# Layer 0's entry, reordered: token tiles turned first, the first head group summed by pairs of K-slices, and two tiles of the second head group summed ahead of the scores

## The chip, the cores and the metric

The kernel runs on one core of one Trainium2 chip. The metric is the device time of one execution in microseconds (us); of the kernel before there are three runs, 1695.23, 1698.65 and 1695.23 us, with a median of 1695.23. The profile is of one more execution on the chip. Engines in the rows: PE (TensorE), PEld (its weight loads), DVE (VectorE), ACT (ScalarE), POOL (GpSimd), SP (SyncE, which issues nearly all loads).

## The reference

Two layers of a transformer block over 512 latent tokens and 256 context tokens of width 1024. Layer 0 has four groups of heads (two with a window, two dense); each group has four query heads, one key head and one value head of width 64. What the change touches is the way into layer 0:

```python
mx = (s_c @ mod_w[l] + mod_b[l])[:, None, :]          # shift, scale, gate ... of the latent tokens
mc = (s_cc @ mod_w[l] + mod_b[l])[:, None, :]         # the same of the context tokens
hx = _rms(x, norm_mix_w[l]) * (1.0 + scx1) + shx1
hc = _rms(ctx, norm_mix_w[l]) * (1.0 + scc1) + shc1
...
qa_x, ka_x, va_x, ... = heads(hx @ w_in, True)        # then RMS norm and rotation of q and k
qa_c, ka_c, va_c, ... = heads(hc @ w_in, False)
```

The change leaves out nothing and computes nothing else.

## The kernel before

**Tiles.** The 768 tokens are six tiles of 128 rows: 4 and 5 are the context, 0 to 3 the latent tokens, taken in the order `CTX_FIRST = (4, 5, 0, 1, 2, 3)`. The width of 1024 is eight K-slices of 128, taken as four pairs. A float32 product is made of three products of rounded parts (high x high, high x low, low x high), so `project` (L465) issues, for one tile and one pair of K-slices, 2 x 3 matmuls of 128x384: the 384 columns are 4 query heads, a key head and a value head. A tile of one head group is 24 matmuls, a head group 144.

**The entry, L1149 to L1214.** `load_x` loads a tile of tokens (512 KB). Its square sum is made on ACT (L1166), the inverse root on POOL (L159, L160), the scaling on DVE (L1167); PE turns it in eight transposes of 128x128 (L1171) into two PSUM banks, and ACT copies both halves into `xT` (L1172). There are two buffers `nh` for the scaled tile, so the third tile's square waits until the first tile has been turned. Beside that, `mod_steps` makes the shift (part 0) and the scale (part 1) of layer 0: for each of four chunks n of 256 columns (two K-slices) and each part it loads two pieces of 512 KB, multiplies them (16 matmuls for a chunk, L182), copies the rows (`modr`, ACT, L185), turns them into columns (L191), and adds them on DVE (L276, L280). `modulated(k)` applies them to a K-slice on DVE (L1184), ACT makes the high part (L1189), DVE or, for the context tokens, POOL the low part (L1190). `weights0` does the same for the weights: a pair of K-slices is three loads (`wir`), a cast on ACT (`wihi`, L498) and a subtraction on DVE or POOL (`wilo`, L499). `start_tile` hands out six buffers under the tag `mw` to mod pieces and to weights; `raw_tile` two others.

**The order.** PE's order is written out by hand between `manual.__enter__` and `manual.__exit__` (first L1176 to L1214); outside, and on the other engines, the scheduler of the language orders instructions by its own timeline, and every engine and SP's queue then run strictly in that order. In the written part, tiles 4 and 5 get all 24 matmuls once all four chunks are on their way. After it the scheduler places the four other tiles.

**What follows.** `in_proj0` copies a summed tile out (`qkv`, ACT, L520), squares it (L440), sums by head (DVE, L442), takes the inverse root on POOL (`rs_q`, L159, L160), multiplies by it on POOL (L523), splits q and k (`qd`, `kd`: ACT L525, L529, DVE L526, POOL L530) and queues two transposes on PE (`turn_q`, `turn_k`, L535, L543). `attend0` then makes scores (`sc`, L578), the softmax and the values. While head group b attends, `quarters` places the products of head group b+1 between its steps, by the table `QUARTS`; one quarter is one pair of K-slices of one tile.

## Time and profile before

| | us |
|---|---|
| three runs | 1695.23, 1698.65, 1695.23 (median 1695.23) |
| span of the profiled execution | 1695.6 |
| PE busy / DVE / ACT / POOL in it | 1631.5 / 1146.7 / 937.0 / 696.4 |
| first product of the first head group begins | 42.91 |
| first scores begin | 77.39 |

The profiled execution's own time is its span, 0.4 us above the median; what else a run's time takes in is not listed. Times below are us from the start of that span. In a row of the timeline stand the start, the length, the engine, the line, the operation, what it writes and reads, the shape and the count; a matmul's length is its way through the array, and matmuls overlap, so their pace is read from starts and counts. In a row of the windows stand the stretch, its length, busy time and count of PE, PEld, DVE, ACT, POOL, then the clock granted to PE (1.00 is full), the busy share of the transfer engines and GB/s.

### The profile page before, as it was taken

The numbers are of one execution on the slowest core, as the hardware profiler recorded it, in microseconds if no ns is written. First come the engines' busy times: TensorE is split into PE (matmuls) and PEld (weight loads), VectorE is DVE, ScalarE is ACT, GpSimd is POOL, SyncE is SP. The second block draws the span as 40 slices with busy tenths as digits, with TensorE's granted clock in tenths as the row PEclk, the third lists the DMA queues.
The fourth block names the chain that finished last, engine by engine and source line by source line (L and its number), as shares of the span: only waits on it lengthen the run. The fifth ranks groups of instructions, "written<-read, shape, count | busy, mean of one in ns | idle before, by whom it ended". The sixth has DMA issues, their size and how long they took to land. (4 is left out here: it accounts for less than half of the span.)

```text
span 1695.6 us, 28585 instructions
## 1 busy us (share of the span) xinstructions
PE 1631.5 (96%) x10390; PEld 1468.6 (87%) x10390; DVE 1146.7 (68%) x2014; ACT 937.0 (55%) x2011; POOL 696.4 (41%) x867
## 2 busy tenths in 40 slices
PE   6999999899999999999999989999999999999998
PEld 3977787677999999998777889999988899999887
DVE  3765656754799887767767656666666598887434
ACT  5565555745456665545554456666666555555320
POOL 2665554321346554412413366666664242221000
PEclk8999999999999999999999999999999999999999
DMA  9222221411455555439966311111112433331431
GB/s 319 69 71 74 70 70 50 164 60 38 129 167 172 164 159 162 134 108 347 296 184 189 99 43 38 48 42 44 50 45 97 125 93 102 111 101 57 137 99 62
DMA packets 218108, 194.64 MB, mean 115 GB/s; under 512 B 20016, under 2 KB 202864, under 8 KB 217968
## 3 DMA queue, kind: packets, MB, share of 16 engines
q1 hardware_dynamic: 217616, 192.62, 36.8%
q8 instruction: 81, 1.33, 0.3%
q14 instruction: 59, 0.48, 0.1%
q10 hardware_dynamic: 352, 0.21, 0.0%
HBM read 179.92 MB, written 12.87 MB: 114 GB/s over the span
## 5 line engine op out<-in xcount | busy, mean ns | idle before, releaser
L901 ACT CAST wbh<-wr 128x512 fp32r<-128x512 f32 x170 | 104.9, 621 | 130.2 <-PE p L933 73.4
L933 PE MATMUL p<-hT,wbh 128*128 128x256 f32 (+1 forms) x752 | 154.5, 299 | 0.0
L465 PE MATMUL inps<-wih,hT 128*128 128x384 f32 x512 | 144.2, 344 | 7.3 <-ACT qkv L677 7.3
L911 POOL TENSOR_TENSOR wbl<-wr,wbh 128x512 fp32r<-128x512 f32 x43 | 60.0, 1396 | 173.6 <-ACT wbh L901 173.6
L933 PEld LDWEIGHTS p<-hT,wbh 128*128 128x128 f32 x752 | 121.9, 191 | 0.2
L911 DVE TENSOR_TENSOR wbl<-wr,wbh 128x512 fp32r<-128x512 f32 x127 | 107.7, 858 | 21.0 <-ACT wbh L901 16.8
L933 PE MATMUL p<-hT,wbl 128*128 128x256 f32 (+1 forms) x376 | 111.9, 298 | 0.0
L933 PE MATMUL p<-t,wbh 128*128 128x384 f32 (+1 forms) x480 | 111.3, 318 | 0.0
L604 POOL TENSOR_SCALAR Pt<-Pt,rc 128x256 f32<-128x256 f32 (+3 forms) x96 | 74.6, 788 | 89.3 <-DVE rc L601 83.1
L231 POOL TENSOR_TENSOR modp<-modp 128x512 f32<-128x512 f32 x40 | 57.4, 1436 | 114.3 <-ACT modp L230 114.3
L465 PEld LDWEIGHTS inps<-wih,hT 128*128 128x128 f32 x512 | 93.3, 188 | 10.6 <-ACT qkv L677 9.7
L933 PE MATMUL p<-hTt,wbh 128*128 128x256 f32 (+1 forms) x480 | 101.0, 302 | 0.0
L887 POOL TENSOR_TENSOR wr<-wr 128x512 f32<-128x512 f32 x40 | 61.6, 1540 | 89.8 <-DVE ws L892 85.8
L933 PE MATMUL p<-b,wbh 128*128 128x384 f32 x368 | 93.8, 336 | 0.2 <-DVE c L961 0.2
L901 ACT CAST wbh<-ws 128x512 fp32r<-128x512 f32 x120 | 69.4, 579 | 43.1 <-PE p L933 29.0
L224 DVE SCALAR_TENSOR_TENSOR ma<-modw,cols,ma 128x256 f32<-128x256 f32 x140 | 89.2, 637 | 2.3
L592 ACT ACTIVATE Pt<-sc,nm 128x256 f32<-128x256 f32 (+3 forms) x96 | 67.6, 707 | 35.3 <-DVE nm L588 16.9
L465 PE MATMUL inps<-wil,hT 128*128 128x384 f32 x256 | 86.0, 336 | 0.0
L933 PEld LDWEIGHTS p<-t,wbh 128*128 128x128 f32 x480 | 82.9, 189 | 0.0
L911 DVE TENSOR_TENSOR wbl<-ws,wbh 128x512 fp32r<-128x512 f32 x120 | 81.7, 681 | 1.7 <-ACT wbh L901 1.6
L933 PEld LDWEIGHTS p<-hTt,wbh 128*128 128x128 f32 x480 | 78.3, 191 | 3.1 <-ACT modp L230 1.6
L230 ACT ACTIVATE modp<-modw,cols 128x256 f32<-128x256 f32 x160 | 68.4, 500 | 18.0 <-POOL ma L236 10.1
(355 smaller groups left out, 5217.9 us busy)
## 6 DMA issues: line engine op xcount, KB each, us to landing
modw<-in_mod_w_dram SPq DMA_DIRECT2D x96, 512.0 KB, 5.2
wr<-in_ffn_w_in_dram SPq DMA_DIRECT2D x176, 256.0 KB, 2.9
wdr<-in_ffn_w_out_dram SPq DMA_DIRECT2D x66, 512.0 KB, 3.7
wir<-in_od_w_in_dram SPq DMA_DIRECT2D x96, 128.0 KB, 2.3
hidm<-hid SPq DMA_DIRECT2D x44, 192.0 KB, 1.9
hr<-hidm SPq DMA_DIRECT2D x22, 192.0 KB, 3.5
x<-in_x_dram SPq DMA_DIRECT2D x8, 512.0 KB, 3.5
wir<-in_ev_w_in_dram SPq DMA_DIRECT2D x16, 256.0 KB, 3.5
```

The source lines that it names most:

```text
L224: nc.vector.scalar_tensor_tensor(acc, w[:, k], scale[k], acc, ALU.mult, ALU.add)
L230: nc.scalar.activation(pr[:, k], w[:, k], AF.Copy, scale=scale[k])
L231: nc.gpsimd.tensor_add(pr[:, 0:2], pr[:, 0:2], pr[:, 2:4])
L465: nc.tensor.matmul(ps, hs[j][:, k, :], ws[k // 2][z][:, k % 2, c0:c1], start=(k, j, z) == (0, 0, 0), stop=(k, j, z) == (KT - 1, 1, 0))
L592: turn["exp"] = nc.scalar.activation(p[:, :n], s, AF.Exp, bias=nm[:, c1], accum_out=sm[:, c1])
L604: nc.gpsimd.tensor_scalar(p[:, :n], p[:, :n], rc[:, hh:hh + 1], 1.0, ALU.mult, ALU.mult)
L887: nc.gpsimd.tensor_sub(w, raw[f, "G1"], w)
L901: nc.scalar.copy(hi, w)
L911: (nc.gpsimd if name == "G2" else nc.vector).tensor_sub(lo, raw[need[n]], f32(hi))
L933: nc.tensor.matmul(ps, w[:, k, :], H[b][h][:, k, :], start=first and k == 0 and q == 0, stop=final and k == 3 and q == 2, skip_group_check ...
```

## The change

The change does the following.

- All six token tiles are loaded ahead of the first mod piece and turned one after the other; the second half of each is copied by DVE and no longer by ACT.
- PE's order is written out by hand from the first transpose on. For each chunk n: its 16 matmuls, its columns, `modulated(n, i)` for the context and the latent tokens, all low parts on DVE, and then the pair of K-slices n of the six tiles. Chunk n+1's matmuls and columns stand between the products of chunk n. Four tiles begin in new places (`acc0`, `acc1` for tiles 4 and 5, the two score buffers for 0 to 3).
- The weights of a pair are loaded one pair at a time, between the chunks' pieces. `mw` has seven buffers; one pair of pieces (chunk 2, part 1) goes to the raw buffers.
- Head group 1's first weights are asked for in the third round; its tiles 4 and 5 are summed in the written part, ahead of the scores, each followed by the transposes of two tiles of head group 0. `QUARTS` for head group 0's attention then places 16 quarters in place of 24.
- The rotation tables and the sinks are placed behind the last low part and the last mod piece.

```diff
+MW = 7
-    def start_mod(n):
-        for part in range(2):
-            mod_chunk(0, part, n, start_tile, start.pool, f"acc{part}", p_sc)
...
+    def chunk_rows(n):
+        chunks[n] = [mod_steps(0, part, n, raw_tile if n == 2 and part else start_tile, start.pool, f"{'tr' if n else 'tr'}{part}", room=("modr", 2))
+                     for part in range(2)]
+        for g in chunks[n]:
+            next(g)
...
-            nc.scalar.copy(xT[:, 4 * g:4 * g + 4, t * P:(t + 1) * P], pt)
+            (nc.vector.tensor_copy if g else nc.scalar.copy)(xT[:, 4 * g:4 * g + 4, t * P:(t + 1) * P], pt)
...
-                (nc.gpsimd if s0 else nc.vector).tensor_sub(lo, xT[:, ks, s0:s1], f32(hi))
+            turn["lows"] = nc.vector.tensor_sub(lo, xT[:, kk, s0:s1], f32(hi))
...
+    xs.update({t: load_x(t) for t in CTX_FIRST[2:]})
+    for t in CTX_FIRST:
+        turned_x(t)
+    chunk_rows(0)
+    units = weights0(0, wp.pool, (nc.vector,), start_tile, ((0,), (1,), (2,), (3,)), True)
+    next(units)
+    chunk_columns(0)
+    for i in (1, 0):
+        modulated(0, i)
+    ws.append(next(units))
...
+    begin(0, *CTX_FIRST[:2])
+    for n in range(1, 4):
+        chunk_rows(n)
+        next(units)
+        if n == 3:
+            units1 = weights0(1, wp.pool, (nc.gpsimd, nc.vector))
+            next(units1)
+        begin(n - 1, *CTX_FIRST[2:4])
+        chunk_columns(n)
+        with behind("lows"):
+            ws.append(next(units))
+        for i in (1, 0):
+            modulated(n, i)
+        begin(n - 1, *CTX_FIRST[4:])
+        begin(n, *CTX_FIRST[:2])
+    with behind("lows"):
+        ws1 = [next(units1) for _ in range(2)]
+    begin(3, *CTX_FIRST[2:])
...
-    for _ in range(2 * NT):
-        quarters(2)
-        turned0()
+    for _ in range(4 * NT):
+        next(proj)
+    ws1 += units1
+    proj = in_proj0(1, ws1, tabs, wp.pool, odd.pool, due)
+    nxt = next(proj)
+    for _ in range(2):
+        for _ in range(4):
+            next(proj)
+        for _ in range(4):
+            due.pop(0)()
+    manual.__exit__(None, None, None)
...
-    QUARTS = ((((2, 2),) * 6), ((2, 2),) * 6, ((2, 2), (2, 2), (4, 2), (2, 4), (2, 2), (0, 0)))
+    QUARTS = (((1, 1), (1, 1), (2, 1), (2, 1), (2, 1), (2, 1)), ((2, 2),) * 6, ((2, 2), (2, 2), (4, 2), (2, 4), (2, 2), (0, 0)))
```

Line numbers of the changed kernel are higher by one up to the entry (L465 becomes L466) and by 7 to 22 behind it.

**PE, the opening.** In the kernel before, the transposes of the six tiles (`npt`), the chunks' matmuls (`mod`) and their columns (`modcol`) are mixed; the stretch from the last tile on reads:

```order
L1171 MATMUL npt<-cst,nh 128x128 x8
L191 MATMUL modcol<-cst,modr 128x2 x2
L182 MATMUL mod<-modw,s_pad 32x256 x12
L191 MATMUL modcol<-cst,modr 128x2 x2
L182 MATMUL mod<-modw,s_pad 32x256 x12
L191 MATMUL modcol<-cst,modr 128x2 x2
L182 MATMUL mod<-modw,s_pad 32x256 x8
L465 MATMUL inps<-wihi,hTc_112 128x384
```

In the changed kernel PE begins:

```order
L145 MATMUL pcol<-cst,rows 128x48
L149 MATMUL pb<-cst,brows 128x96
L1180 MATMUL npt<-cst,nh 128x128 x48
L183 MATMUL mod<-modw,s_pad 32x256 x16
L192 MATMUL modcol<-cst,modr 128x2 x4
L466 MATMUL inps<-wihi,hTc_112 128x384
```

All 48 transposes stand ahead of the first chunk, and the first product behind one chunk in place of four.

**ACT, the rounds.** Here `wihi` is the high part of a pair of weights and `wir` its load, `modr` the rows of a chunk, `hTc0` and `hT0` the high parts of the context and latent tokens. Before, from the second part of chunk 2's rows on:

```order
L185 COPY modr_357<-mod_344 128x256
L185 COPY modr_379<-mod_366 128x256
L498 CAST wihi_422<-wir_396 128x768
L1189 CAST hT0_110<-xT_210 128x512
L498 CAST wihi_436<-wir_400 128x768
L1189 CAST hTc0_112<-xT_210 128x512
```

In the changed kernel, from behind the first chunk's high parts to those of the third:

```order
L499 CAST wihi_377<-wir_352 128x768
L499 CAST wihi_470<-wir_445 128x768
L186 COPY modr_335<-mod_322 128x256
L186 COPY modr_350<-mod_337 128x256
L1191 CAST hTc0_112<-xT_124 128x512
L1191 CAST hT0_110<-xT_124 128x512 x2
L186 COPY modr_428<-mod_415 128x256
L186 COPY modr_443<-mod_430 128x256
L499 CAST wihi_571<-wir_538 128x768
L499 CAST wihi_609<-wir_542 128x768
L499 CAST wihi_613<-wir_546 128x768
L1191 CAST hTc0_112<-xT_124 128x512
```

The casts of the second and third pair (`wir_352`, `wir_445`) now stand ahead of chunk 1's rows; those of the fourth pair and of head group 1's first two (`wir_538`, `wir_542`, `wir_546`) ahead of chunk 2's high parts. SP issues `wir_445` into the buffer of `wir_352` and `wir_538` into that of `wir_445`, so each waits for the low part of the pair before it on DVE, and that stands behind the round's low parts of the tokens. `wir_542` and `wir_546` follow in SP's queue.

**POOL, the first tiles' rotation.** `qy` are the rotated heads of a tile, `rs_q` their inverse roots (two instructions, the second against `neghalf`), `kd` a tile's key. Before, from the first tile's inverse root to the second tile's key:

```order
L160 TENSOR_TENSOR rs_q_562<-rs_q_562,neghalf_92 128x5
L160 TENSOR_TENSOR rs_q_582<-rs_q_582,neghalf_92 128x5
L159 TENSOR_SCALAR rs_q_637<-qss_635 128x5
L523 TENSOR_TENSOR qy_565<-qy_565,rs_q_562 128x320
L523 TENSOR_TENSOR qy_585<-qy_585,rs_q_582 128x320
L160 TENSOR_TENSOR rs_q_637<-rs_q_637,neghalf_92 128x5
L530 TENSOR_TENSOR kd_572<-qy_565,kd_572 128x128
L499 TENSOR_TENSOR wilo_867<-wir_862,wihi_866 128x768
L530 TENSOR_TENSOR kd_592<-qy_585,kd_592 128x128
```

In the changed kernel, from the low part of head group 1's third pair to the second tile's key:

```order
L500 TENSOR_TENSOR wilo_809<-wir_804,wihi_808 128x768
L161 TENSOR_TENSOR rs_q_695<-rs_q_695,neghalf_92 128x5
L522 COPY vv_667<-qkv_732 128x64
L160 TENSOR_SCALAR rs_q_715<-qss_713 128x5
L531 TENSOR_TENSOR kd_685<-qy_678,kd_685 128x128
L160 TENSOR_SCALAR rs_q_739<-qss_737 128x5
L524 TENSOR_TENSOR qy_698<-qy_698,rs_q_695 128x320
L161 TENSOR_TENSOR rs_q_715<-rs_q_715,neghalf_92 128x5
L161 TENSOR_TENSOR rs_q_739<-rs_q_739,neghalf_92 128x5
L522 COPY vv_667<-qkv_756 128x64
L524 TENSOR_TENSOR qy_718<-qy_718,rs_q_715 128x320
L531 TENSOR_TENSOR kd_705<-qy_698,kd_705 128x128
```

The low part of the weights has moved ahead of the second tile's inverse root, and two more inverse roots and a multiplication ahead of its key.

More of the change, by code (lines that the diff above doesn't have):

```diff
@@ L1192, in backbone, with begin @@
-    ws, begun, first = [], {}, CTX_FIRST[:2]
-    for k in range(6):
-        modulated(k)
-        if k % 2:
-            ws += islice(units, 1)
-    for i in range(0, 4, 2):
+        for kk in [slice(ks[0], ks[0] + 2)] if i else [slice(k, k + 1) for k in ks]:
+            hi, lo = (cols_T(j, s0, s1)[:, kk, :] for j in range(2))
+            turn["started"] = nc.scalar.copy(hi, xT[:, kk, s0:s1])
+            turn["lows"] = nc.vector.tensor_sub(lo, xT[:, kk, s0:s1], f32(hi))
+    def begin(n, *tiles):
+        for t in tiles:
+            project(begun[t], t, ws, 0, 384, range(2 * n, 2 * n + 2))
@@ L1198, in backbone @@
+    xs.update({t: load_x(t) for t in CTX_FIRST[2:]})
[8 more added lines that the diff above has]
+    ws.append(next(units))
+    for i, t in enumerate(CTX_FIRST[:2]):
+        begun[t] = acc_tile("inps", 384, one=i)
+    for i in range(2, 6, 2):
         sc = p_sc.pool.tile([P, 1024], F32, name="inps", tag="sc", bufs=2)
```

68 lines of the change are left out of this document (23 added, 45 removed).

## Prediction

> **What bounds the kernel now.** I read the page's slices first, then the windows, then PE's timeline of the entry. The page shows PE's busy tenths and its clock in 40 slices of 42.4 us:
>
> ```profile
> PE   6999999899999999999999989999999999999998
> PEclk8999999999999999999999999999999999999999
> ```
>
> PE is the bound everywhere but in the first slice. Only there and in the head groups behind it can this change act. The windows of that stretch:
>
> ```profile
> 0.00:20.00 20.00, 8.96 (x74) 4.60 (x74) 2.85 (x7) 10.79 (x21) 3.22 (x12) 1.00 0.96 327
> 20.00:40.00 20.00, 15.05 (x109) 9.87 (x110) 11.10 (x23) 11.10 (x23) 5.34 (x8) 0.68 1.09 329
> ...
> 0.00:42.90 42.90, 26.65 (x202) 15.76 (x202) 15.95 (x36) 23.77 (x46) 8.56 (x20) 0.82 1.00 319
> 42.90:77.40 34.50, 33.04 (x199) 32.22 (x195) 25.89 (x50) 16.93 (x38) 21.13 (x27) 0.98 0.28 81
> ...
> 80.00:100.00 20.00, 18.63 (x133) 15.85 (x132) 11.47 (x45) 12.74 (x42) 15.85 (x30) 1.00 0.17 57
> 100.00:120.00 20.00, 18.25 (x142) 14.55 (x140) 14.13 (x41) 13.88 (x37) 12.25 (x19) 1.00 0.33 93
> ```
>
> Up to 42.9 us the transfers run without a pause (share 1.00, 319 GB/s) and PE does 26.65 us of work, partly at a low clock. From 42.9 to the first scores at 77.4 PE is busy 33.04 of 34.5 us, and behind that it idles 1.4 to 1.8 us in 20. So the entry waits for loads, and then PE has everything it needs. PE's timeline:
>
> ```profile
> 11.28 1.06 PE L1171 MATMUL npt<-cst,nh 128*128 128x128 f32 x4
> ...
> 14.85 1.07 PE L182 MATMUL mod<-modw,s_pad 128*32 128x256 f32 x16
> ...
> 20.36 1.94 PE L1171 MATMUL npt<-cst,nh 128*128 128x128 f32 x8 [2.74 <-DVE modc L276]
> ...
> 26.81 1.94 PE L1171 MATMUL npt<-cst,nh 128*128 128x128 f32 x8 [1.05 <-DVE nh L1167]
> 28.68 1.08 PE L182 MATMUL mod<-modw,s_pad 128*32 128x256 f32 x8
> 29.69 1.50 PE L1171 MATMUL npt<-cst,nh 128*128 128x128 f32 x8
> ...
> 37.91 1.94 PE L182 MATMUL mod<-modw,s_pad 128*32 128x256 f32 x16 [1.12 <-DVE modc L276]
> ...
> 42.91 1.56 PE L465 MATMUL inps<-wihi,hTc 128*128 128x384 f32 x4
> 44.30 0.50 PE L191 MATMUL modcol<-cst,modr 128*128 128x2 f32 x4
> ...
> 77.39 0.70 PE L578 MATMUL sc<-kT,qt 128*128 128x256 f32 x4
> ```
>
> The most that could be won is what PE loses up to 77.4: 17.7 us idle (77.4 - 26.65 - 33.04) and some 8 us of low clock.
>
> **Step 1: the transposes first.** They no longer share PE with the chunks, but a tile's loop is a chain: square, inverse root, scaling, eight transposes, and two tiles are in flight (two buffers `nh`).
>
> ```profile
> 6.59 1.04 ACT L1166 ACTIVATE nh<-x 128x1024 f32<-128x1024 f32 x1
> ```
>
> ```profile
> 8.68 0.75 DVE L1167 TENSOR_SCALAR nh<-x,rs_n 128x1024 f32<-128x1024 f32 x1 [1.08 <-POOL rs_n L160]
> ...
> 40.83 0.16 DVE L276 TENSOR_TENSOR modc<-modcol,bcol 128x4 f32<-128x4 f32 x1 [2.97 <-PE modcol L191]
> 41.22 1.65 DVE L1184 TENSOR_SCALAR xT<-xT,aff,modc 128x256 f32<-128x256 f32 x4
> 42.79 0.95 DVE L499 TENSOR_TENSOR wilo<-wir,wihi 128x768 fp32r<-128x768 f32 x1
> 43.66 0.69 DVE L1190 TENSOR_TENSOR hT<-xT,hT 128x512 fp32r<-128x512 f32 x1
> ```
>
> From the start of a square to its scaled tile are 2.84 us (6.59 to 9.43). The half that DVE now copies stands ahead of the scaling; I give it 0.69, as for the other 128x512 DVE operation. So a pair of tiles takes 2.84 + 0.69 + the transposes of its first tile, 1.94 at the low clock or about 1.07 at the full one: 5.5 or 4.6 us. The first pair starts at 9.5, and the last transpose ends at 24.4 (low clock throughout) or 21.7 (full from the second pair on). The loads are no limit: the six tiles and what comes ahead of them are 3.5 MB, 11 us at 327 GB/s.
>
> The clock decides between the two:
>
> ```profile
> 30.00:30.50 0.50, 0.50 (x4) 0.50 (x3) 0.00 (x0) 0.26 (x1) 0.00 (x0) 0.50 1.10 350
> 30.50:31.00 0.50, 0.50 (x6) 0.50 (x5) 0.00 (x0) 0.20 (x1) 0.00 (x0) 0.92 1.09 342
> ```
>
> It rose at 30.5, after a stretch from 26.81 in which PE worked without a pause and two thirds of the work were transposes; so here transposes count towards the clock, and the full clock can come in during them. The Trainium skill says otherwise ("TensorE: Matmul & The Clock Gate", Part 4: PE-mode transpose): in transpose mode the full clock "doesn't engage", which speaks against 48 transposes in a row. By that rule the low-clock sums below hold, by the rows either may; the runs here cannot settle it ahead of the change.
>
> **Step 2: chunk 0 to the first product.** 16 matmuls (1.94 or 1.07), then ACT's copy, the columns (0.50), and on DVE 40.83 to 42.87 plus one low part, 2.73.
>
> ```profile
> L1172 ACT COPY xT<-npt 128x512 f32<-128x512 f32 x12 | 6.7, 586 | 5.8 <-PE npt L1171 5.8
> L498 ACT CAST wihi<-wir 128x768 fp32r<-128x768 f32 x6 | 4.9, 832 | 0.4 <-DMA wir<-in_ev_w_in_dram 0.4
> L185 ACT COPY modr<-mod 128x256 f32<-128x256 f32 x8 | 2.9, 368 | 7.4 <-PE mod L182 3.8 <-PE modcol L191 3.6
> L1189 ACT CAST hTc<-xT 128x512 fp32r<-128x512 f32 x4 | 2.5, 613 | 0.0
> ```
>
> 24.4 + 1.94 + 0.37 + 0.50 + 2.73 and some handing over: 30.1, or 26.5 at the full clock. The first product thus comes 13 to 16 us earlier than at 42.91. That is the gain on paper; steps 3 to 5 ask how much of it reaches the scores.
>
> **Step 3: chunk 1's columns (call their end C).** Two chains meet there. On PE: 12 products, whose pace is 0.35 at the low clock (four from 42.91 to 44.30) and 0.17 at the full one:
>
> ```profile
> 60.00:68.00 8.00, 8.00 (x48) 8.00 (x47) 0.36 (x1) 1.00 0.19 53
> ```
>
> PE has just idled 3 us, so I take 4.2; then 16 matmuls (1.5 as a middle), 12 products (2.1), columns (0.5): 38.4 from the late start, 34.8 from the early one. The other chain is ACT's order: chunk 1's rows are copied only behind the casts of the second and third weight pair. The second pair lies behind 9.6 MB of loads, 29.2 us at 329 GB/s; cast 0.83 and low part 0.95 give 31.0, or, from the late start, 30.1 + 1.3 for DVE's other low parts + 0.95 = 32.4. Only then is the third pair's load issued.
>
> ```profile
> 56.82 2.94 SPq L491 DMA_DIRECT2D wir<-in_ev_w_in_dram x6
> ```
>
> ```profile
> DMA to landing us min/median/max: 2.8/3.5/6.2
> ```
>
> Three issues begin over 1.0 us (0.49 each), and the last lands 2.8 to 3.5 after its issue, about 4.1 in all; cast 0.83, two copies 0.74, columns 0.5. C is 37.2 (early) or 38.6 (late): the early start gives most of its lead back here.
>
> **Step 4: from C to the first tile's sum (T, the end of tiles 4 and 5).** A round at PE's own pace is 36 products (6.2), 16 matmuls (1.07), columns (0.5) and about 0.85 idle until DVE's 2.9 us are done, 8.6. In the second round ACT casts three weight pairs ahead of chunk 2's context tokens. The first of them waits for its buffer until C + 2.9 + 1.3 + 0.95 = C + 5.1; nine issues of 0.49 start their last at C + 9.1; landing 2.8, cast 0.83, high part 0.61, low part 0.69: the products of chunk 2 start at C + 14.0 in place of C + 11.5. T is C + 14.0 + 8.6 + 2.1 = C + 24.7, so 61.9 or 63.3. In the kernel before, both tiles were copied out at 58.40:
>
> ```profile
> 58.40 0.86 ACT L520 COPY qkv<-inps 128x384 f32<-128x384 f32 x2 [3.57 <-PE inps L465]
> ```
>
> So the rotation on POOL starts 3 to 5 us later than before, though products start 13 us earlier, because six tiles are summed side by side.
>
> **Step 5: from T to the first scores.** PE still has 24 products of head group 0 and 24 of head group 1's tile 4 (8.3 us), then turns tiles 4 and 5. POOL's rows:
>
> ```profile
> 67.31 1.84 POOL L499 TENSOR_TENSOR wilo<-wir,wihi 128x768 fp32r<-128x768 f32 x1
> 69.11 0.64 POOL L530 TENSOR_TENSOR kd<-qy,kd 128x128 fp32r<-128x128 f32 x1
> 69.70 0.23 POOL L521 COPY vv<-qkv 128x64 f32<-128x64 f32 x1
> ...
> 74.17 1.16 POOL L160 TENSOR_TENSOR rs_q<-rs_q,neghalf 128x5 f32<-128x5 f32 x1
> 75.30 0.45 POOL L530 TENSOR_TENSOR kd<-qy,kd 128x128 fp32r<-128x128 f32 x1
> 75.71 0.72 POOL L523 TENSOR_TENSOR qy<-qy,rs_q 128x320 f32<-128x320 f32 x1
> ```
>
> The third pair of head group 1 is loaded when the second's low part is done on DVE, at T + 0.2; it lands at T + 4, is cast by T + 4.8, and POOL makes its low part by T + 6.7. Behind it stand, in order, the second tile's inverse root (1.16), a copy and two short rows (0.6), the first tile's key (0.45), a multiplication (0.72), two inverse roots (2.3), a copy and a multiplication (0.95), the second tile's key (0.45): T + 13.4. Its turning and the copy of the keys take another 0.9: scores at T + 14.3. PE has run dry by T + 10. That gives 76.2 or 77.6, against 77.39. Up to there PE has done 168 products and two tiles' turns, before 164 and three; the two differences cancel.
>
> **Step 6: behind the scores.** 16 quarters are left for the attention in both orders, since the scheduler had already pulled tiles 4 and 5 of head group 1 ahead of most of it. POOL's late keys of tiles 0 to 3 are covered by the 47 products behind the first scores (8.0 us). I put this at zero, bounded by half the idle of the two windows from 80 to 120, 1.6 us either way. The low parts of the context move from POOL to DVE, 4 x 0.69, inside the 2.9 of a round and counted there; a seventh `mw` buffer, the sinks and the tables cost nothing as long as SP's queue is not the wait, and step 4 is where it would be.
>
> **Sum.** -0.2 to +1.2 us of gain at the scores, the middle 0.5. On the profiled span of 1695.6 that is 1695.1; the span stands 0.4 above the median, so 1694.7.
>
> **The rivals.**
>
> *The rounds run at PE's pace.* If the weight loads land in time for ACT's casts, step 3 ends at 34.8 to 38.4 and T is C + 22.3; POOL then has its weights too and loses 2 us less in step 5. Scores at 69 to 73, a gain of 4 to 8; I take 6, 1689.2. For it: the transfer engines are free by then (share 0.28 from 42.9 on). Against it: the waits are for buffers and low parts, not for bandwidth. It decides if the last of the three casts ahead of chunk 2 ends by C + 10.
>
> *The cover is spent early.* Between the first scores and the first transposed probabilities the new order places 71 products, the old 45. 26 products (4.5 us) are then missing beside later steps of the attention. If those steps are bound by ACT, DVE and POOL and PE stands for that time, the gain turns into 1694.7 + 4.5 = 1699.2. For it: POOL was busy 15.85 of 20 us from 80 to 100. Against it: from 100 on POOL has 40% to spare. It decides if PE's idle from 95 to 140 exceeds 3 us in 20.
>
> *The change doesn't do what it says* I exclude: the orders of both programs show it.
>
> **How the numbers follow.** About 0.2%, 3.4 us, is what a measurement of this kernel can tell from no change; two of the three runs agree and the third stands 3.42 above. My forecast has 0.44, with its bounds (1.4 from the clock, 1.6 from step 6) mostly within 0.2%: 0.32 same, 0.07 faster, 0.05 slower. PE's pace has 0.34: 0.30 faster, 0.04 same. The spent cover has 0.22: 0.19 slower, 0.03 same. Together 0.37, 0.39, 0.24. The range reaches from 1688.0 (a gain of 7) to 1699.5, the slow rival's point; the forecast's own is 1692 to 1697.
>
> **What would show it.** Right: first product at 26 to 31; ACT's cast of chunk 2's context tokens directly behind three weight casts, PE idle some 3 us ahead of chunk 2's products; `qkv` first copied after 61; PE idle some 4 us ahead of the first scores, at 75 to 79. Wrong: scores before 73, or no wait of ACT for `wir`; or PE busy less than 17 of 20 us from 95 to 140.

## The result and the profile after

The changed kernel takes 1715.63 us (median of 4 runs, 1711.89 to 1717.24), the kernel before 1695.23 (4 runs, 1692.94 to 1698.65): a ratio of 1.0116, 95% interval 1.0101 to 1.0131. It is slower by 20 us. The forecast was no change, its range ended at 1699.5, and the cause has to be looked for.

The profiled execution of the changed kernel took 1715.41 us with a span of 1712.8; in all profiled executions below a run's time stands 1.7 to 2.6 us above its span. The span of 1695.6 of before was therefore an execution of some 1697 to 1698 us, and not one 0.4 above the median, as the prediction took it. So the two traces lie 17.2 us apart where the medians lie 20.4 apart; what follows explains those 17.2.

**Where it is lost.** The page of the changed kernel, in slices of 42.8 us:

```profile
PE   5889999899999999999999989999999999999998
...
PEclk8889999999999999999999999999999999999999
```

In these tenths nothing has changed behind the fifth slice. The attention's output copies tell the same. ACT's timeline of the kernel before, the first and the tenth copy:

```profile
93.97 0.40 ACT L625 COPY o<-av 128x256 f32<-128x256 f32 x1
...
207.02 0.37 ACT L625 COPY o<-av 128x256 f32<-128x256 f32 x1 [0.96 <-PE av L623]
```

and of the changed one:

```profile
113.81 0.38 ACT L626 COPY o<-av 128x256 f32<-128x256 f32 x1
...
223.86 0.37 ACT L626 COPY o<-av 128x256 f32<-128x256 f32 x1 [0.96 <-PE av L624]
```

The lag is 19.8 us at the first copy and 16.8 at the tenth, and it stays at 16.8 up to the last. The first products of the FFN begin 16.7 us later; PE's row before, then of the changed kernel:

```profile
431.59 0.52 PE L933 MATMUL p<-hT,wbh 128*128 128x384 f32 x2
...
448.27 0.52 PE L934 MATMUL p<-hT,wbh 128*128 128x384 f32 x2
```

So all is lost ahead of the first output, and 3 us of it are given back behind it.

The windows show what PE loses. A window's loss is what PE stands idle (length minus busy time) and what a low clock costs it (busy time times one minus the clock). Changed kernel:

```profile
0.00:20.00 20.00, 7.35 (x35) 5.43 (x35) 6.81 (x12) 12.44 (x22) 4.89 (x17) 0.93 0.96 321
20.00:40.00 20.00, 15.29 (x112) 11.29 (x112) 7.82 (x15) 5.91 (x10) 0.55 (x1) 0.82 0.85 266
...
40.00:70.00 30.00, 27.56 (x176) 24.15 (x177) 14.43 (x31) 9.49 (x19) 2.10 (x1) 0.83 0.33 96
70.00:80.00 10.00, 9.21 (x53) 8.68 (x51) 8.13 (x23) 5.66 (x12) 7.73 (x9) 1.00 0.33 83
80.00:100.00 20.00, 13.23 (x66) 12.23 (x66) 12.74 (x36) 10.85 (x29) 17.20 (x30) 0.74 0.16 51
```

Kernel before, the same stretches from 40 us on:

```profile
40.00:70.00 30.00, 29.75 (x178) 28.28 (x178) 21.38 (x41) 14.05 (x28) 16.15 (x18) 0.93 0.28 77
70.00:80.00 10.00, 8.54 (x54) 7.83 (x53) 9.12 (x23) 6.44 (x18) 7.41 (x13) 1.00 0.33 106
80.00:100.00 20.00, 18.63 (x133) 15.85 (x132) 11.47 (x45) 12.74 (x42) 15.85 (x30) 1.00 0.17 57
```

From 40 to 70 the changed kernel loses 2.4 us of idle time and 27.56 x 0.17 = 4.7 of clock, before 0.2 and 2.1; from 70 to 80 it is 0.8 against 1.5; from 80 to 100 it is 6.8 and 13.23 x 0.26 = 3.4, before 1.4 and nothing. In all 18.1 against 5.2: 12.9 of the 16.8 us of lag stand in these 60 us, in two places, the rounds (4.8, from 40 to 70) and the wait ahead of and behind the first scores (8.8, from 80 to 100); from 70 to 80 it loses 0.7 less. Up to 40 us both lose the same, by windows of 1 us 21.7 and 21.5, although the first product now begins at 29.76 and not at 42.91. That is the first lesson of the two traces: a landmark came 13 us earlier and PE had not got further, because the transposes and the chunks' matmuls that used to fill this time now stand ahead of it or behind it.

**The rounds.** PE's timeline of the changed kernel:

```profile
20.00 3.98 PE L1180 MATMUL npt<-cst,nh 128*128 128x128 f32 x16 [1.54 <-DVE nh L1176]
...
29.76 0.45 PE L466 MATMUL inps<-wihi,hTc 128*128 128x384 f32 x1 [1.93 <-ACT hTc L1191]
...
40.49 1.41 PE L192 MATMUL modcol<-cst,modr 128*128 128x2 f32 x8 [2.25 <-ACT modr L186]
...
48.90 1.93 PE L183 MATMUL mod<-modw,s_pad 128*32 128x256 f32 x32
...
57.84 0.51 PE L466 MATMUL inps<-wihi,hTc 128*128 128x384 f32 x1 [1.76 <-ACT hTc L1191]
...
84.64 0.51 PE L536 MATMUL qpt<-identr,qd 128*128 128x128 f32 x4 [2.11 <-DVE qd L527]
...
86.96 0.37 PE L544 MATMUL kpt<-identr,kd 128*128 128x128 f32 x1 [1.72 <-POOL kd L531]
87.79 1.41 PE L579 MATMUL sc<-kT,qt 128*128 128x256 f32 x4 [0.46 <-ACT kT L545]
90.84 0.69 PE L466 MATMUL inps<-wihi,hTc 128*128 128x384 f32 x1 [1.64 <-ACT qkv L521]
```

A chunk's matmuls are 32 records in 1.93 us even at the full clock, and its columns, in another row, take 0.95. The waits at 40.49 and 57.84 are for ACT, and ACT's own timeline shows what ACT waits for:

```profile
39.33 0.83 ACT L499 CAST wihi<-wir 128x768 fp32r<-128x768 f32 x1 [6.46 <-DMA wir<-in_ev_w_in_dram]
40.07 0.64 ACT L186 COPY modr<-mod 128x256 f32<-128x256 f32 x2
...
54.18 0.84 ACT L499 CAST wihi<-wir 128x768 fp32r<-128x768 f32 x1 [2.13 <-DMA wir<-in_ev_w_in_dram]
56.44 0.83 ACT L499 CAST wihi<-wir 128x768 fp32r<-128x768 f32 x1 [1.42 <-DMA wir<-in_ev_w_in_dram]
57.18 0.61 ACT L1191 CAST hTc<-xT 128x512 fp32r<-128x512 f32 x1
...
70.58 0.48 ACT L521 COPY qkv<-inps 128x384 f32<-128x384 f32 x1 [0.88 <-PE inps L466]
```

The rows of L499 are casts of weights that wait for a load and stand in ACT's queue ahead of what PE needs next: the first ahead of chunk 1's rows (`modr`), the other two, with a third at 51.22, ahead of the high part of chunk 2's context tokens (`hTc`). Their loads, in SP's queue:

```profile
33.89 1.39 SPq L492 DMA_DIRECT2D wir<-in_ev_w_in_dram  x3
46.72 7.29 SPq L492 DMA_DIRECT2D wir<-in_ev_w_in_dram  x9
```

The nine loads of 46.72 take 7.29 us to issue, where nine at 0.49 would take 4.4.

**The scores.** Tiles 4 and 5 are copied out from 70.58 on (58.40 before), the first scores begin at 87.79 (77.39). From 82.5 on PE has nothing left to sum and turns q and k as POOL and DVE hand them over, and when it goes on to sum, at 90.84, its products come 0.32 apart up to 95.5.

### The profile page after: what moved, and what is told of

The parts are those of the page before. It is cut to its first block, busy times and chain, and to the rows that moved or that the text cites. A ratio compares the mean times of both kernels' runs of the same rounds, so it can differ in the third digit from the quotient of the medians.

```text
span 1712.8 us, 28587 instructions
## 1 busy us (share of the span) xinstructions
PE 1638.6 (96%) x10390; PEld 1475.4 (86%) x10390; DVE 1148.5 (67%) x2024; ACT 936.0 (55%) x2005; POOL 690.6 (40%) x863
## 5 line engine op out<-in xcount | busy, mean ns | idle before, releaser
L466 PE MATMUL inps<-wih,hT 128*128 128x384 f32 x512 | 144.2, 344 | 7.7 <-ACT qkv L678 7.7
L466 PEld LDWEIGHTS inps<-wih,hT 128*128 128x128 f32 x512 | 93.3, 188 | 11.0 <-ACT qkv L678 10.1
L225 DVE SCALAR_TENSOR_TENSOR ma<-modw,cols,ma 128x256 f32<-128x256 f32 x140 | 87.8, 627 | 2.3
L466 PE MATMUL inps<-wil,hT 128*128 128x384 f32 x256 | 86.0, 336 | 0.0
L466 PE MATMUL inps<-wihi,hT 128*128 128x384 f32 x256 | 76.6, 354 | 1.3 <-DVE modc L277 1.3
```

The costliest lines, as they stand in the source:

```text
L225: nc.vector.scalar_tensor_tensor(acc, w[:, k], scale[k], acc, ALU.mult, ALU.add)
L466: nc.tensor.matmul(ps, hs[j][:, k, :], ws[k // 2][z][:, k % 2, c0:c1], start=(k, j, z) == (0, 0, 0), stop=(k, j, z) == (KT - 1, 1, 0))
```

## The experiments

A lag is that of the first FFN product against the 431.59 of the kernel before; T is the first copying out of tiles 4 and 5; the loss is PE's from 40 to 100 us, worked out as above from the three windows. Behind that first FFN product the executions differ by up to 3.0 us either way (old_entry's span is 2.5 us longer than that of before, its lag 5.5), so that a lag and a time need not agree better than that.

| kernel | time, us | T | scores | loss 40 to 100 | lag |
|---|---|---|---|---|---|
| before | 1695 | 58.4 | 77.4 | 5.2 | 0 |
| changed | 1715.6 | 70.6 | 87.8 | 18.1 | 16.7 |
| old_tail | 1708.7 | 68.6 | 86.7 | 16.6 | 12.3 |
| old_entry | 1702.1 | 56.0 | 81.2 | 9.6 | 5.5 |
| casts_late | 1710.7 | 64.3 | 81.3 | 13.6 | 16.5 |
| warm | 1713.5 | 67.3 | 85.4 | 9.4 | 16.6 |
| late_old_tail | 1705.5 | 66.7 | 83.4 | 12.0 | 11.1 |
| few | 1702.2 | 58.5 | 83.0 | 10.0 | 4.5 |
| few_pool | 1700.8 | 56.7 | 77.6 | 8.6 | 3.1 |
| old_side | 1701.5 | 62.1 | 79.5 | 11.6 | 3.5 |
| x_first | 1698.6 | 58.2 | 76.3 | 7.8 | 1.5 |
| t_first | 1694.3 | 54.9 | 73.5 | 5.6 | -2.1 |

The loss of *warm* isn't comparable with the others, since it counts the matmuls added there as work.

**The two halves apart.** The first question was which half of the change costs. *old_tail* keeps the new entry and takes back the way to the scores:

```diff
-        if n == 3:
-            units1 = weights0(1, wp.pool, (nc.gpsimd, nc.vector))
-            next(units1)
...
+    manual.__exit__(None, None, None)
...
-    for _ in range(4 * NT):
-        next(proj)
-    ws1 += units1
...
+    for _ in range(2 * NT):
+        quarters(2)
+        turned0()
...
-    QUARTS = (((1, 1), (1, 1), (2, 1), (2, 1), (2, 1), (2, 1)), ...
+    QUARTS = ((((2, 2),) * 6), ...
```

> The new entry with the old way from the entry to the scores (head group 1's weights loaded behind the entry, its tiles placed by the scheduler, 24 quarters in QUARTS). Theory 1 (the rounds of the entry cost the time: each round waits and drops the clock, and six tiles summed side by side end 12 us later): most of the loss stays, 1708 to 1714 us, first scores after 84. Rival A (the two tiles and turns written ahead of the scores are the cost): 1695 to 1700, first scores before 80.

1708.71 us, ratio 1.0080 (1.0061 to 1.0099), first scores at 86.7. *old_entry* is the opposite, the old entry with the new lines from the diff above:

> The old entry with the new way to the scores (two tiles of head group 1 and the turns written ahead of the scores, 16 quarters left in QUARTS). Theory 1: tiles 4 and 5 are copied out at 58 as before, POOL has made their keys by the time PE has done 192 products, PE stays busy, the scores begin at about 83 and the time is 1694 to 1700. Rival A (the written tail is the cost): 1709 to 1716, with PE idle ahead of the scores as in the changed kernel.

1702.10 us, ratio 1.0044 (1.0025 to 1.0063), scores at 81.2. So neither half is innocent: the entry costs 14 us, the tail 7 to 8, and together that is what the change costs. old_tail came as theory 1 said. old_entry fell between the two ranges: the tail has a price of its own that theory 1 gave as 5 at most.

But old_entry's entry is not quite the old one. PE's written order now reaches up to the scores, so the scheduler no longer places tiles 0 to 3. In the kernel before, it has PE sum products of theirs from 44.66 on, up to the last columns; in old_entry PE stands at this place, waiting for ACT. The columns before, then in old_entry, and old_entry's window:

```profile
48.57 0.50 PE L191 MATMUL modcol<-cst,modr 128*128 128x2 f32 x4
...
46.03 0.61 PE L191 MATMUL modcol<-cst,modr 128*128 128x2 f32 x4 [1.58 <-ACT modr L185]
...
40.00:70.00 30.00, 27.47 (x152) 25.71 (x152) 22.84 (x47) 13.40 (x28) 14.66 (x19) 0.88 0.29 77
```

From 40 to 70 old_entry loses 5.8 us, the kernel before 2.3. So of the 4.4 us that old_entry loses more by 100 us, 3.5 stand ahead of the tail's own work.

The new tail does not cause the wait at the scores. With the old tail PE stands as long; its windows and the wait in its timeline:

```profile
70.00:80.00 10.00, 6.40 (x36) 5.86 (x34) 7.62 (x18) 4.36 (x10) 9.33 (x13) 1.00 0.27 79
80.00:100.00 20.00, 16.49 (x83) 15.38 (x84) 12.40 (x39) 13.37 (x40) 15.61 (x28) 0.74 0.16 53
```

```profile
80.08 0.51 PE L536 MATMUL qpt<-identr,qd 128*128 128x128 f32 x4 [2.53 <-DVE qd L527]
```

3.6 us idle from 70 to 80, and 3.5 idle with 4.3 of clock from 80 to 100, are 11.4, against 11.0 in the changed kernel.

**ACT's order.** *casts_late* leaves PE's program alone and moves only ACT's casts of weights behind the rows that PE waits for:

```diff
-        with behind("lows"):
+        with behind("lows", "modr"):
             ws.append(next(units))
...
-    with behind("lows"):
+    with behind("lows", "started"):
         ws1 = [next(units1) for _ in range(2)]
```

> The changed kernel with ACT's order alone changed: each weight pair's cast stands behind the chunk's own rows, and head group 1's casts behind the last round's high parts. Theory 1: ACT's waits for weight loads (2.25 us of PE ahead of chunk 1's columns, 1.76 ahead of chunk 2's products) and the low clock behind them go; tiles 4 and 5 end 4 to 6 us earlier, at 66 to 68, and the time is 1709 to 1712. Rival A: 1714 to 1717, since the path lies in the tail.

1710.74 us, ratio 1.0093 (1.0074 to 1.0111), T at 64.3. The time is what theory 1 said, 5 us less, though the two intervals overlap a little. (The profiled execution is the slowest of its four, 1715.33; its lag of 16.5 is that execution's. Its granted clock was 0.50 in three stretches of over 3 us between 144 and 217 us, where the changed kernel has one.) The windows show the rounds cured, and a new wait where the first one went:

```profile
40.00:70.00 30.00, 29.41 (x215) 26.07 (x215) 18.93 (x43) 12.33 (x24) 5.72 (x7) 1.00 0.42 130
70.00:80.00 10.00, 5.80 (x27) 4.70 (x27) 7.33 (x18) 4.74 (x11) 9.61 (x13) 0.81 0.49 145
80.00:100.00 20.00, 16.34 (x88) 14.96 (x88) 12.78 (x44) 12.48 (x39) 16.06 (x31) 0.75 0.01 2
```

The loss of the rounds falls from 7.1 to 0.6 us, that from 70 to 100 rises from 11.0 to 13.0. A shorter entry reaches the wait for the rotation sooner and stands in it.

**The clock.** *warm* adds 224 small bf16 matmuls (the trace holds 224 records more than that of the changed kernel; the expectation's 160 is a miscount) that add zero to tile 4's sum, or write a bank that nobody reads, where PE rests:

```diff
+    def warm(n, dst, into=True):
+        for _ in range(n):
+            nc.tensor.matmul(dst, identb, zerob if into else identb, start=not into, stop=not into)
...
         begin(n - 1, *CTX_FIRST[2:4])
+        if n == 1:
+            warm(32, begun[4][:, :P])
         chunk_columns(n)
...
+        if n < 3:
+            warm(24, begun[4][:, :P])
         begin(n, *CTX_FIRST[:2])
...
         for _ in range(4):
+            warm(16, dst, False)
             due.pop(0)()
```

> The changed kernel with 160 small bf16 matmuls that add zero or write a bank that nobody reads, put where PE waits (ahead of chunk 1's columns, of the products of chunks 1 and 2, and among the turns ahead of the scores), so that PE does not rest. Theory 1: the clock stays up from 40 to 62 and from 82 to 96, where about 21 us were at half speed; products that are 0.32 apart come 0.17 apart, and the time is 1706 to 1711. Rival B (the clock is off the path: the rounds are set by DVE, ACT and loads, and the low clock only fills waiting time): 1714 to 1718.

1713.49 us, ratio 1.0105 (1.0089 to 1.0121). The clock stayed up in the rounds, and less so at the scores:

```profile
40.00:60.00 20.00, 19.58 (x199) 17.00 (x200) 10.15 (x22) 7.24 (x14) 2.17 (x1) 1.00 0.45 138
80.00:100.00 20.00, 15.49 (x161) 14.95 (x160) 10.42 (x32) 10.91 (x31) 15.26 (x26) 0.83 0.03 11
```

From 40 to 60 it is 1.00 (0.78 in the changed kernel), from 80 to 100 it is 0.83 (0.74), and T comes 3.3 us earlier. But only 2 us arrive at the end, within the spread of the runs. The time lies in neither range, nearer to rival B's: of the 3.3 us at T, 2.4 are left at the scores and 2 at the end. How much the added matmuls themselves cost was not measured, so this is no bound on what the low clock takes.

**Both edits.** *late_old_tail* takes casts_late and old_tail together.

> The changed kernel with both edits at once: the casts behind the chunk's rows, and the old way to the scores. In six kernels so far the first scores came 17.0 to 19.0 us after tiles 4 and 5 were first copied out wherever PE was not the bound, with POOL busy 15 to 17 of 20 us in between. Theory 1 (refined: the copying out, T, starts a chain of some 18 us on POOL, and what PE has left to sum at T decides how much of it PE stands still): T at 62 to 65, scores at 80 to 83, the two savings add, 1701 to 1706 us. Rival C (one common wait behind both, so that only the larger saving counts): 1707 to 1711.

1705.52 us, ratio 1.0063 (1.0038 to 1.0088): the savings of 5 and 7 us nearly add (the sum would be 1703.8), so they are two costs and not one. Beside old_tail, the later casts are worth 3 us here and not 5, and the intervals overlap again. T (66.7) and the scores (83.4) came later than the expectation had them.

**Two tiles in a round, and not six.** *few* is late_old_tail with rounds that sum tiles 4 and 5 alone; tiles 0 to 3 follow whole, where the scheduler places them:

```diff
         chunk_rows(n)
         next(units)
-        begin(n - 1, *CTX_FIRST[2:4])
+        begin(n - 1, *CTX_FIRST[:2])
         chunk_columns(n)
...
-        begin(n - 1, *CTX_FIRST[4:])
-        begin(n, *CTX_FIRST[:2])
...
-    begin(3, *CTX_FIRST[2:])
+    begin(3, *CTX_FIRST[:2])
```

> As late_old_tail, but the rounds sum only tiles 4 and 5; tiles 0 to 3 are summed whole behind them. Theory 1: T comes at 52 to 57 because a round then holds 12 products and not 36, PE still has 96 products of head group 0 (16.5 us) for the 18 us of POOL's chain, the scores begin at 71 to 75 and the time is 1690 to 1697. Rival D (the loss comes from loading and turning the tokens first, or from the rounds as such, whatever is summed in them): 1701 to 1706, as in late_old_tail.

1702.21 us, ratio 1.0039 (1.0021 to 1.0058); T at 58.5, scores at 83.0. A miss for theory 1 in its numbers: T came no earlier than before, 8 us earlier than in late_old_tail, and 3.3 us of time followed. So about a third of what was left in late_old_tail may be the summing side by side; the intervals overlap.

*old_side* tries that part alone, on the kernel before: tiles 4, 5, 0 and 1 side by side.

```diff
     for k in range(2, KT, 2):
-        for t in first:
+        for t in CTX_FIRST[:4]:
             project(begun[t], t, ws, 0, 384, range(k, k + 2))
```

> The kernel before with one edit: four tiles (4, 5, 0, 1) and not two are summed side by side by pairs of K-slices. Theory 1: T moves from 58.4 to 65 to 67, the scores to 83 to 85, with 48 products of head group 0 left at T and the rest taken from head group 1; PE stands still 2 to 6 us ahead of the scores; 1697 to 1702 us. Rival D (the order of the sums does not matter as long as PE has all it needs): 1693 to 1696.

1701.46 us, ratio 1.0046 (1.0031 to 1.0062). T comes 3.7 us later and the scores 2.1, less than expected, since the scheduler had already placed some products of other tiles there; the loss from 70 to 100 is 7.6 us against 2.8, and the time 6.7 us more. So the order of the sums matters although PE has all that it needs: rival D falls.

*x_first* tries another part alone: the six token tiles loaded ahead of the first mod piece in the kernel before, and the first chunks placed behind the tiles' transposes.

```diff
-    xs = {t: load_x(t) for t in CTX_FIRST[:2]}
-    start_mod(0)
-    start_mod(1)
-    xs.update({t: load_x(t) for t in CTX_FIRST[2:]})
+    xs = {t: load_x(t) for t in CTX_FIRST}
...
+    for n in range(3):
+        start_mod(n)
```

> The kernel before with one edit: all six token tiles are loaded ahead of the first mod piece and turned as they come. Theory 1: the last load of the entry lands as before, so the first product stays at 41 to 45 and the time at 1693 to 1698. Rival D (loading the tokens first costs by itself): over 1700.

1698.64 us, ratio 1.0025 (1.0015 to 1.0036): 4 us for this order, between the two ranges expected. The first product, at 41.03, comes 1.9 us earlier and T, at 58.2, is unmoved, so the cost does not come by way of these. PE stands 1.9 us more from 80 to 100 (16.68 us busy, before 18.63).

**Does the time follow T?** In twelve of the seventeen kernels the scores came 16.5 to 19.0 us behind T. In the other five it was 20.9 to 27.8; in two of these, few and free_old (below), PE's order has 187 and 192 products ahead of the scores in place of 168. *t_first* moves T the other way, in the kernel before: tiles 0 to 3 may not be summed ahead of the last product of tiles 4 and 5.

```diff
+    summed = nc.cur_bb.bb.instructions[-1]
     manual.__exit__(None, None, None)
...
-                project(ps, t, ws, 0, 384, range(k, k + 2))
+                with tc.issue_after(summed):
+                    project(ps, t, ws, 0, 384, range(k, k + 2))
```

> The kernel before with one edit: no product of tiles 0 to 3 is issued ahead of the last one of tiles 4 and 5. Theory 1 (T, the copying out of tiles 4 and 5, sets the start of the rotation's chain, and the time follows T): T at 52 to 56 in place of 58.4, first scores at 70 to 74 in place of 77.4, and the lag of the attention output against the kernel before is -2 to -5 us: 1690 to 1693. Rival E (PE is the bound from 43 on, so the order of its work does not matter): 1694 to 1697, within 0.1% of the kernel before.

1694.30 us, ratio 0.9996 (0.9985 to 1.0006). The scores in PE's timeline, and ACT's first and tenth output copies:

```profile
73.49 0.70 PE L579 MATMUL sc<-kT,qt 128*128 128x256 f32 x4
```

```profile
93.75 0.37 ACT L626 COPY o<-av 128x256 f32<-128x256 f32 x1
...
205.19 0.37 ACT L626 COPY o<-av 128x256 f32<-128x256 f32 x1 [0.96 <-PE av L624]
```

T moved by -3.5 and the scores by -3.9, as theory 1 said, but the first output by -0.2 and the time not at all, as rival E said. The scores followed T; as far as these runs go, the time follows a late T, when PE then has nothing to sum, and not an early one.

*pool_free* takes all low parts of head group 1's weights from POOL, in the kernel before:

```diff
-    units = weights0(1, wp.pool, (nc.gpsimd, nc.vector))
+    units = weights0(1, wp.pool, (nc.vector,))
```

> The kernel before with one edit: all low parts of head group 1's weights are made by DVE, none by POOL (1.84 us of POOL at 67.3, and another one). Theory 1 in its strong form (the 18 us from T to the scores are POOL's work, one operation after the other): the scores come 1 to 2 us earlier at the same T, 1692 to 1695. If the 18 us are a chain of waits among the engines and not POOL's load: scores at 76.5 to 78, 1694 to 1696.

1693.31 us, ratio 0.9988 (0.9979 to 0.9997), scores 16.8 us behind T in place of 19.0. POOL's load is part of the chain, and this is the one version whose interval lies below the kernel before, by 2 us and only just. *t_pool*, both edits:

> The two edits of t_first and pool_free at once. Theory 1: T at 52 to 56, scores at 69 to 72, 1689 to 1692. Rival E: 1694 to 1697.

1693.77 us, ratio 0.9996 (0.9984 to 1.0008): the scores at 72.5, and again nothing in the time.

**The tail's own price.** *tail_one* is old_entry with one tile of head group 1 written ahead of the scores and not two, and 20 quarters left:

```diff
-    for _ in range(2):
-        for _ in range(4):
-            next(proj)
-        for _ in range(4):
-            due.pop(0)()
+    for _ in range(4):
+        next(proj)
+    for _ in range(4):
+        due.pop(0)()
```

> The old entry with one tile, and not two, of head group 1 written ahead of the scores, 20 quarters left in QUARTS. If the tail costs by what PE must do ahead of the scores (24 products are 4.1 us) and lacks as filler behind them: half of old_entry's loss of 8 us, so 1697 to 1700, scores at 78 to 80. If it costs by the hand-written turns as such: 1701 to 1703 as in old_entry.

1702.51 us, ratio 1.0045 (1.0031 to 1.0058): not half the price but all of it. That speaks for the hand-written order, and in part rightly: from 40 to 70 tail_one loses 7.3 us, old_entry 5.8 and the kernel before 2.3, at the place shown above. *free_old* and *free_tail* end PE's written order ahead of the tail (the same lines, `manual.__exit__` earlier), with the old and with the new entry:

> As old_entry (old entry, new tail with 16 quarters in QUARTS), but PE's order behind the first two tiles is left to the scheduler. If the hand-written order of PE is the tail's cost: 1694 to 1697. If it is the work placed ahead of the scores and missing behind them (QUARTS): 1700 to 1704, as old_entry with 1702.

> The changed kernel, but PE's order behind the last product of head group 0 is left to the scheduler. If the hand-written order is the tail's cost: 1706 to 1710, as old_tail with 1708.7. If it is QUARTS: 1713 to 1717, as the changed kernel.

1709.06 us, ratio 1.0082 (1.0062 to 1.0101), and 1712.76, ratio 1.0101 (1.0085 to 1.0117). Neither lies in a range expected. With the old entry the scheduler's order of the same work is 7 us worse than the written one, although it loses only 3.6 us from 40 to 70; with the new entry it is 3 better, with intervals that overlap. So with the old entry the hand-written order costs at the entry's end and saves more behind it: it is not the price as a whole. What all kernels with the new tail have in common is read from the order of PE's instructions: they have summed 237 to 240 products when the first output is made, the kernel before 216; at the fifth it is 264 to 270 against 264. In old_entry ACT's first output copy stands here,

```profile
104.22 0.38 ACT L625 COPY o<-av 128x256 f32<-128x256 f32 x1
```

10.2 us behind the 93.97 of before; at the fifth copy, where both have summed about as much, 6.2 are left. So work is done earlier, and only some of its time is given back, 5.4 being left at the tenth copy. The 3.5 us lost ahead of 70 may be the larger part of these; t_first loses 2.3 us there and gets them back, so this is argued only. In the new entry all products of head group 0 are written with either tail, so that part is missing; there T comes 2.0 us later with the new tail, whose first casts stand in the third round (three ahead of chunk 2's context tokens, two in old_tail). The rest of the tail's price is open: PE's idle time behind the first output does not show it.

Last, *few_pool*, few with the edit of pool_free:

> As few, with the low parts of head group 1's weights on DVE and not on POOL. In few, PE rests 3.9 us and runs 2.9 us' worth at a low clock between 60 and 80, waiting for q, k and a copy of the first tiles, while POOL makes a low part for 2.27 us ahead of the second tile's inverse root. If that is what is left in few: scores before 79, PE's loss from 60 to 80 at most half, 1697 to 1700. If not: 1701 to 1703.

1700.82 us, ratio 1.0029 (1.0014 to 1.0043). The scores come at 77.6, 5.4 us earlier than in few, as expected, but the time falls by 1.4 only, which the runs hardly tell from nothing. PE's loss from 60 to 80 was to be halved; it goes from 8.2 to 7.6 us, so most of what PE loses there has another cause than POOL's low part.

## Why the prediction was wrong, step by step

The likeliest case was "no change". The chance of slower by over 0.2% was 0.24, 0.19 of it for the spent cover, which is not the mechanism found. What failed are four terms of the sum: the mechanisms of steps 3 to 5 are in the trace as they were described, but their sizes were too small, each to the same side, 10.4 us together against the scores of the kernel before, and step 6, put at zero, took another 6.4. These make the 16.8 us of lag.

- **Step 1** said that the transposes end at 21.7 to 24.4; they end at 24.0. **Step 2** said 26.5 to 30.1 for the first product; it begins at 29.76. Both held, at the late end.
- **The Trainium skill's rule** that in transpose mode the full clock "doesn't engage" ("TensorE: Matmul & The Clock Gate", Part 4: PE-mode transpose) is not what this case shows: behind a stretch of transposes alone, from 9.91 on, eight of them came in 1.07 us, twice the pace of the sixteen before them and of the sixteen at 20.00. The trace calls them matmuls; whether they are the mode that the page means, no run here shows. Rows and windows of the changed kernel:

```profile
9.91 3.87 PE L1180 MATMUL npt<-cst,nh 128*128 128x128 f32 x16 [0.36 <-DVE nh L1176]
15.31 1.07 PE L1180 MATMUL npt<-cst,nh 128*128 128x128 f32 x8 [1.53 <-DVE nh L1176]
...
20.00:24.00 4.00, 3.98 (x16) 2.96 (x16) 2.22 (x3) 2.00 (x3) 0.55 (x1) 0.51 1.10 348
...
44.00:48.00 4.00, 4.00 (x15) 4.00 (x14) 2.65 (x4) 0.76 (x2) 0.00 (x0) 0.52 0.05 17
```

- **Step 3** gave C, the end of chunk 1's columns, as 37.2 to 38.6; it is 40.49 + 1.41 = 41.9. The chain was the one named: ACT's cast of the third weight pair ahead of chunk 1's rows. But its load was asked for at 33.89, 1.5 to 2.9 us later than the sum had it (31.0 or 32.4), and cast at 39.33, 5.4 us and not 4.1 from the first issue to the cast, and the columns took 1.41 and not 0.5. This is the first mis-sized term, 3.3 to 4.7 us.
- **Step 4** gave T as C + 24.7; it is C + 28.7. The three casts ahead of chunk 2's tokens are there, and the products of chunk 2 begin at 57.84, C + 15.9 in place of C + 14.0. The nine loads took 7.29 us to issue, since buffers for the second and third pair only come free with chunk 2's matmuls at 48.90 to 50.83 (SP's waits there name PE's `mod`, for 2.3 us); "nine issues of 0.49" left that wait out. The other 2.0 are in the round behind it, where a chunk is 1.93 and not the 1.07 that the prediction took for it (it counted 16 rows of the profile where there are 32), and where products come 0.3 to 0.4 apart for 3.7 us. Mis-sized by 4.0.
- **Step 5** gave the scores as T + 14.3 and PE as dry from T + 10: they came at T + 17.2, and PE was dry from T + 12. POOL's two rows that bound the chain:

```profile
76.90 1.83 POOL L500 TENSOR_TENSOR wilo<-wir,wihi 128x768 fp32r<-128x768 f32 x1
...
86.46 0.45 POOL L531 TENSOR_TENSOR kd<-qy,kd 128x128 fp32r<-128x128 f32 x1
```

  The low part ended at T + 8.2 and not T + 6.7, and from there to the second tile's key POOL took 8.2 us and not 6.7. Mis-sized by 2.9. The three errors make 10.2 to 11.6, the scores' delay against the forecast.
- **"The two differences cancel"**, at the end of step 5, held as a count: the changed kernel too has summed 168 products when its scores begin. So the sum would have stood if the scores had come at 76 to 78; they came 10.4 us late, with nearly the same work done. What the landmarks hid is that each wait of steps 3 to 5 is idle time of the engine that bounds the kernel; PE's loss from 40 to 100, 12.9 us more, shows it at once. The "8 us of low clock" up to 77.4, on which no term rests, come to 5.5 when counted as busy time at a low clock.
- **Step 6** put what lies behind the scores at 0, bounded by 1.6. The lag of 10.4 at the scores is 16.8 at the tenth output copy, so 6.4 us were added there. Some 4.5 of them stand in PE's rows right behind the scores: these took 1.41 us in place of 0.70, then PE waited 1.64 for ACT's copy of a summed tile, and the 14 products from 90.84 to 95.48 took 4.6 at the low clock, where 0.17 apart they take 2.4. The lag of 19.8 at the first output counts 26 products more that stand ahead of it (71 in place of 45). In old_entry, which has these 26 products too, only 1.6 us are added between the scores (3.8) and the tenth copy (5.4), so they alone do not explain step 6's error.
- **The rivals.** "The rounds run at PE's pace" was to hold if the last of the three casts ended by C + 10; it ended at C + 15.4. It had 0.34 and falls. "The cover is spent early" had the right sign. Its own test, an idle time of over 3 us in 20 from 95 to 140, failed (0.8 from 100 to 120 and 2.2 from 120 to 140), so it is not what happened.
- **The signs of being right** came in part: the first product at 29.76, `qkv` behind 61, and PE idle some 4 us ahead of the scores (2.11, 1.72 and 0.46). The scores at 75 to 79 did not come, and PE's wait ahead of chunk 2's products was 1.76 and not some 3.

What is shown: the entry and the tail each cost, 14 and 7 to 8 us, by old_tail and old_entry. With ACT's casts moved, PE's loss in the rounds goes (7.1 to 0.6 us), and 3 to 5 us of the time with it (casts_late, late_old_tail). In the kernel before, four tiles side by side cost 7 us (old_side) and the order of loads and transposes 4 (x_first). What is argued only: that summing six tiles side by side takes some 3 us of the new entry (few against late_old_tail, whose intervals overlap, and whose tiles 0 to 3 are also placed in another way), and that x_first's 4 us are the same 4 there. What the low clock takes is not bounded: warm gained 2 us. Open: by what way x_first's order costs when T does not move, what takes the rest of the tail's price, and what the parts of the entry cost that no run tried alone: low parts and copies moved to DVE, the seventh buffer, and where the tables and sinks stand.

## What to carry to other kernels

Price a reordering by the time that the bounding engine loses, idle and at a low clock, in each stretch, and not by when its first product or its first scores come: here the first product came 13 us earlier and the kernel became 20 us slower. Where an engine works strictly in order, look for the instruction that waits for a load in front of one that the bounding engine needs; two lines that moved such casts were worth 3 to 5 us. The count of idle time and clock has its limits: in casts_late and warm it is far from the lag. A written order also takes away what a scheduler had placed in a gap: look at the place where it begins to hold. Summing several outputs side by side finishes all of them late: ask what is left to do when the first one enters a long chain on other engines, since a landmark that comes late costs, and one that comes early need not win anything.

## What the hardware showed that was not expected

PE's clock fell after shorter rests than expected. PE's timeline of the changed kernel, on both sides of the wait of 1.76 us at 57.84:

```profile
55.57 0.34 PE L466 MATMUL inps<-wilo,hT 128*128 128x384 f32 x1
55.75 0.34 PE L466 MATMUL inps<-wihi,hT 128*128 128x384 f32 x1
...
58.15 0.52 PE L466 MATMUL inps<-wilo,hTc 128*128 128x384 f32 x1
```

Products that had come 0.18 us apart took 0.52 each behind it, and they came 0.3 to 0.4 apart up to 61.3, with no wait listed between. Behind the wait of 2.25 us at 40.49 the clock was 0.52 from 44 to 48, where PE worked without a pause. The Trainium skill gives an idle window of about 3.4 us for the fall ("TensorE: Matmul & The Clock Gate", Part 1: The HAM clock gate); in this trace rests of 1.76 and 2.25 us went ahead of it, while the full pace of 15.31 came behind a rest of 1.53. No run here measures what decides.

DVE was slower in a round beside POOL. The same four operations of DVE took 1.65 us in one round and 3.16 in the next, in which POOL made a low part of weights:

```profile
42.33 1.65 DVE L1187 TENSOR_SCALAR xT<-xT,aff,modc 128x256 f32<-128x256 f32 x4
...
54.33 3.16 DVE L1187 TENSOR_SCALAR xT<-xT,aff,modc 128x256 f32<-128x256 f32 x4
```

```profile
55.10 2.10 POOL L500 TENSOR_TENSOR wilo<-wir,wihi 128x768 fp32r<-128x768 f32 x1 [34.55 <-ACT wihi L499]
```

The prediction's 2.9 us for DVE in a round left no room for that. It is one round of one trace, and no run tries POOL's part alone.
